# Three-product matmuls of an encoder block: the matmul on the weights' low part moved to the end of each K tile, and the K loop of a plain weight pair moved outside the loop over the accumulators

## The chip, the cores and the metric

The kernel runs on one core of a Trainium2 chip, as one program in one launch. The metric is the time of that program on the device, in microseconds (us). Each kernel's time is the median of several runs; the profile is taken of one execution by the hardware profiler.

## The reference

One layer of a bidirectional encoder, batch 1, 256 tokens, model width 2048, all in float32. Cut to what matters:

```python
h = rms_norm(x, g_mix)                       # x: 256 x 2048
c_q, c_kv, k_rope, dq, dk, dv = split(h @ w_in)
out_mla  = mla_attention(...)                # 8 heads, from c_q (512 wide), c_kv (256), k_rope (64)
out_diff = diff_attention(...)               # 4 heads, two softmaxes each, minus lam
x = x + concatenate([out_mla, out_diff]) @ w_out      # 2048 x 2048
x = x + cross_attention(rms_norm(x), rms_norm(mem))   # 4 heads into 256 memory tokens
hf = rms_norm(x, g_ffn)
x = x + (silu(hf @ w_gate) * (hf @ w_up)) @ w_down    # hidden width 5632
return rms_norm(x, g_final)
```

The inputs are random; no mask is used anywhere.

## The kernel before, in words

*Precision.* TensorE gets every operand as two float32r tiles, a high part `h` (the value rounded by a cast on ScalarE, L107) and a low part `l` (the value minus the high part, a subtraction on VectorE, L108). A product of two such operands is three matmuls into the same accumulator, written by `mm(o, l, r)`: high stationary x high moving (L99), high stationary x low moving (L100), low stationary x high moving (L101). The stationary operand is always a 128 x 128 block of activations, the moving one a 128 x 512 block of weights. In the names, `wh` and `wl` are the weights' high and low part, and `mixT_h`, `x2n_h`, `hT_h`, `forms_h` with their `_l` partners are activations.

*Wide projections.* The output projection, the gate, up and down products of the feed-forward part and their like run in `wide_project` (L254). It computes 256 tokens x 1024 columns in four accumulators of 128 x 512 in PSUM, `accs[tt][oc]`: tt is the half of the tokens, oc the half of the columns. The weights come in pairs of K tiles (two times 128 rows of 1024 columns), 1 MB a pair by one DMA into a tile `wraw` of a pool of three. `kinds` gives each pair a letter:

- A plain pair ("P") is split as two halves, one for each K tile, into `wh` and `wl` (pool `wp`, four buffers each). Then each accumulator takes its two K tiles, three matmuls each: 24 matmuls.
- A summed pair ("W") is computed with seven products in place of eight. VectorE adds blocks of the weights into `tsum` (L287, L291, L292), which are split too, and the activations have a set of prepared combinations, `forms` (`summed_pair`, L239: four small additions into `sums`, L245 to L248, and three splits). Four products go into extra PSUM tiles Q1, Q5, Q7, Q6 that are shared by all summed pairs of the projection, three go straight into an accumulator: 21 matmuls. After the last summed pair, `leave(Q)` takes the four Q tiles out of PSUM with one ScalarE copy and four VectorE additions or subtractions (L358 to L361 in `wide_add`).

`order` sets the order of the pairs in a projection. At its end, `join` combines each accumulator with what `leave` produced (VectorE, L340 in `wide_result`, L364 in `wide_add`). `wide_add` adds into the residual: its accumulators begin as a ScalarE copy of the residual (L261), which needs the PSUM bank free; the banks of accumulators and of Q tiles change places from one projection to the next (`banks.reverse()`).

```python
w = [split_blocks(raw[:, 2 * k:2 * k + 2, :]) for k in range(2)]   # plain pair, L271
for tt in range(NT):
    for oc in range(2):
        for k in range(2):
            mm(accs[tt][oc], pairs[i].at(k, tt), w[k][:, oc, :], ...)
```

*What sets the order.* The program is written in the order of the computation, and the Tile framework then schedules it with a timeline of its own (`schedule_with_timeline_sim=True`): each engine's instructions are put into a fixed list, in which a matmul may pass others of the source. On the chip an engine works off its list in order and waits, where it must, on semaphores. So both the code and the scheduler decide what stands behind what on TensorE (PE), VectorE (DVE) and ScalarE (ACT). The loads of `wraw` are issued by SyncE (SP) in program order.

*Stages in time.* Input projection and attention to about 230 us, output projection and cross-attention to about 460, then the feed-forward part: gate and up products of 1024 columns each, the hidden tile transposed by TensorE, and three groups of down projections of two halves each, the last of which ends the program with the final norm.

Of the kernel before, what the change touches and what calls it, by code (L numbers as in the profile page):

```python
# [15 lines left out]
AF = mybir.ActivationFunctionType  # L16
ALU = mybir.AluOpType
# [4 lines left out]
NT = S // P  # L22
# [16 lines left out]
GU_KINDS = "PPWPWPWP"  # L39

# [40 lines left out]
def encoder_block(ctx: ExitStack, tc: tile.TileContext, a, out):  # L81
    nc = tc.nc
# [14 lines left out]
    def mm(o, l, r, start, stop, seeded=False):  # L97

        nc.tensor.matmul(o, l.h, r.h, start=start, stop=False, skip_group_check=seeded)  # L99
        nc.tensor.matmul(o, l.h, r.l, start=False, stop=False, skip_group_check=seeded)  # L100
        nc.tensor.matmul(o, l.l, r.h, start=False, stop=stop, skip_group_check=seeded)  # L101

    last_split, last_cast = [None], [None]
# [119 lines left out]
    def split_blocks(src, pool=None):  # L223
        w = w_tile(src.shape[1], pool)
        split_into(w, src)
        return w
# [27 lines left out]
    def wide_project(pairs, src, order, kinds, leave, join, closed=(0, 1), before=None, seed=None):  # L254

        accs = [[acc_tile() for _ in range(2)] for _ in range(NT)]
# [7 lines left out]
        Q = {}  # L264
        for n, i in enumerate(order):
            stop = n == len(order) - 1
# [58 lines left out]
    def wide_result(pairs, src, order, kinds):  # L325
# [16 lines left out]
        wide_project(pairs, src, order, kinds, leave, join)  # L342
# [747 lines left out]
```

## Time and profile before

| quantity | value |
|---|---|
| time, median of 3 runs | 1142.07 us (1141.78 to 1142.09) |
| time of the profiled execution | 1141.65 us |
| its span | 1139.8 us |
| instructions in it | 14403 |
| mean granted TensorE clock | 0.998 of full speed |
| bytes moved by DMA | 222.13 MB, mean 195 GB/s |

The profiled execution is one more run; its time is 1.85 us above its span, the stretch from its first to its last recorded instruction. Busy time is the time in which an engine executes, not the time in which it is needed: an engine that is busy 85% of the span may never be what the others wait for. Weight loads (PEld) run on TensorE beside its matmuls, so the two shares of PE and PEld don't add up. In rows of single instructions the columns are start, length, engine, line of the kernel, operation, output <- inputs, with buffer numbers left out; a wait, where there is one, stands in brackets at the end with the partner that ended it. The row of the chain of waits gives what the end of the program hung on, followed back: PE for 98% of the span.

```profile
PE 98%; issue 1%; ACT 0%; DVE 0%; POOLq 0%; POOL 0%; ACTq 0%
```

### The profile page before, as it was taken

The numbers are of one execution on the slowest core, as the hardware profiler recorded it, in microseconds if no ns is written. First come the engines' busy times: TensorE is split into PE (matmuls) and PEld (weight loads), VectorE is DVE, ScalarE is ACT, GpSimd is POOL, SyncE is SP. The second block draws the span as 40 slices with busy tenths as digits, with TensorE's granted clock in tenths as the row PEclk, the third lists the DMA queues.
The fourth block names the chain that finished last, engine by engine and source line by source line (L and its number), as shares of the span: only waits on it lengthen the run. The fifth ranks groups of instructions, "written<-read, shape, count | busy, mean of one in ns | idle before, by whom it ended". The sixth has DMA issues, their size and how long they took to land.

```text
span 1139.8 us, 14403 instructions
## 1 busy us (share of the span) xinstructions
PE 1130.6 (99%) x5390; PEld 946.4 (83%) x5390; DVE 973.2 (85%) x1322; ACT 667.5 (59%) x965; POOL 58.6 (5%) x75
## 2 busy tenths in 40 slices
PE   9999999999999999999999999999999999999997
PEld 7888888888788888888888888888888888888886
DVE  7788766878896777989898988998998898999895
ACT  7755455567566555665565555565554564665663
POOL 5910000000001000000000000000000000000000
PEclk9999999999999999999999999999999999999999
DMA  9655333546567444455556556556555555565553
GB/s 362 241 195 185 124 125 139 181 149 224 191 227 259 156 161 179 161 211 189 212 194 219 185 191 218 185 190 216 185 187 220 201 205 190 191 247 196 195 181 129
DMA packets 35494, 222.13 MB, mean 195 GB/s; under 512 B 4321, under 2 KB 5601, under 8 KB 11105
## 3 DMA queue, kind: packets, MB, share of 16 engines
q1 hardware_dynamic: 33696, 216.60, 52.9%
q0 software_dynamic: 864, 3.15, 0.8%
q10 hardware_dynamic: 864, 1.47, 0.4%
q8 instruction: 42, 0.69, 0.2%
q14 instruction: 28, 0.22, 0.1%
HBM read 219.11 MB, written 2.10 MB: 194 GB/s over the span
## 4 chain that ended last, share of the span: by engine, by line
PE 98%; issue 1%; ACT 0%; DVE 0%; POOLq 0%; POOL 0%; ACTq 0%
PE acc L99 26%; PE acc L101 26%; PE acc L100 26%; PE q L100 4%; PE q L99 4%; PE q L101 4%; PE pt L502 2%; PE ppt L650 1%; PE psc L100 1%; PE psc L101 1%; PE psc L99 1%; PE acckv L99 0%; PE acckv L101 0%; PE acckv L100 0%; PE pt L922 0%
## 5 line engine op out<-in xcount | busy, mean ns | idle before, releaser
L107 ACT CAST wh<-wraw 128x1024 fp32r<-128x1024 f32 (+2 forms) x401 | 389.8, 989 | 283.2 <-PE acc L101 219.5
L108 DVE TENSOR_TENSOR wl<-wraw,wh 128x1024 fp32r<-128x1024 f32 (+2 forms) x401 | 455.3, 1148 | 88.8 <-ACT wh L107 86.8
L107 ACT CAST wh<-tsum 128x1024 fp32r<-128x1024 f32 (+1 forms) x98 | 98.0, 1006 | 73.1 <-PE acc L101 29.7
L108 DVE TENSOR_TENSOR wl<-tsum,wh 128x1024 fp32r<-128x1024 f32 (+1 forms) x98 | 113.6, 1165 | 19.5 <-ACT wh L107 19.5
L100 PE MATMUL acc<-wl,x2n_h 128*128 128x512 f32 x320 | 124.5, 390 | 0.0
L101 PE MATMUL acc<-wh,x2n_l 128*128 128x512 f32 x320 | 123.9, 389 | 0.0
L99 PE MATMUL acc<-wh,x2n_h 128*128 128x512 f32 x320 | 108.2, 390 | 0.0
L100 PE MATMUL acc<-wl,x0T_h 128*128 128x512 f32 x224 | 88.5, 395 | 0.0
L101 PE MATMUL acc<-wh,x0T_l 128*128 128x512 f32 x224 | 88.2, 394 | 0.0
L99 PE MATMUL acc<-wh,x0T_h 128*128 128x512 f32 x224 | 86.9, 396 | 0.0
L100 PE MATMUL q<-wl,forms_h 128*128 128x512 f32 x191 | 74.3, 389 | 0.0
L101 PE MATMUL q<-wh,forms_l 128*128 128x512 f32 x191 | 74.1, 389 | 0.0
L100 PE MATMUL acc<-wl,hT_h 128*128 128x512 f32 x188 | 73.3, 392 | 0.0
L101 PE MATMUL acc<-wh,hT_l 128*128 128x512 f32 x188 | 72.4, 389 | 0.0
L101 PEld LDWEIGHTS acc<-wh,x2n_l 128*128 128x128 f32 x320 | 60.1, 188 | 12.4
L100 PEld LDWEIGHTS acc<-wl,x2n_h 128*128 128x128 f32 x320 | 60.1, 188 | 12.3
L99 PEld LDWEIGHTS acc<-wh,x2n_h 128*128 128x128 f32 x320 | 59.9, 188 | 12.3
L99 PE MATMUL q<-wh,forms_h 128*128 128x512 f32 x191 | 66.7, 389 | 0.0
L99 PE MATMUL acc<-wh,hT_h 128*128 128x512 f32 x188 | 64.5, 391 | 0.0
L100 PE MATMUL acc<-wl,forms_h 128*128 128x512 f32 x162 | 62.5, 389 | 0.0
L101 PE MATMUL acc<-wh,forms_l 128*128 128x512 f32 x162 | 62.4, 389 | 0.0
L99 PE MATMUL acc<-wh,forms_h 128*128 128x512 f32 x162 | 61.3, 389 | 0.0
(402 smaller groups left out, 2247.9 us busy)
## 6 DMA issues: line engine op xcount, KB each, us to landing
wraw<-in_w_gate SPq DMA_DIRECT2D x44, 1024.0 KB, 4.8
wraw<-in_w_up SPq DMA_DIRECT2D x44, 1024.0 KB, 4.8
wraw<-in_w_dn SPq DMA_DIRECT2D x41, 1024.0 KB, 4.8
wraw<-in_w_in SPq DMA_DIRECT2D x24, 1024.0 KB, 4.8
wraw<-in_w_out SPq DMA_DIRECT2D x16, 1024.0 KB, 4.8
wraw<-in_w_in_lat SPq DMA_DIRECT2D x5, 832.0 KB, 7.2
wraw<-in_w_xk SPq DMA_DIRECT2D x4, 1024.0 KB, 5.4
wraw<-in_w_xq SPq DMA_DIRECT2D x4, 1024.0 KB, 5.9
```

Source lines behind the costliest of these rows:

```text
L99: nc.tensor.matmul(o, l.h, r.h, start=start, stop=False, skip_group_check=seeded)
L100: nc.tensor.matmul(o, l.h, r.l, start=False, stop=False, skip_group_check=seeded)
L101: nc.tensor.matmul(o, l.l, r.h, start=False, stop=stop, skip_group_check=seeded)
L107: last_cast[0] = nc.scalar.copy(out=dst.h, in_=src).ins
L108: last_split[0] = nc.vector.tensor_tensor(out=dst.l, in0=src, in1=dst.h.bitcast(F32), op=ALU.subtract).ins
L502: nc.tensor.transpose(out=pt[:, j * P:(j + 1) * P], in_=src[:, j * P:(j + 1) * P], identity=ident)
L650: nc.tensor.transpose(out=pt[:, kt * S + tt * P:kt * S + (tt + 1) * P], in_=p[:, tt, kt * P:(kt + 1) * P], identity=ident)
```

## The change

Three things, all in the order in which matmuls are written; the set of matmuls, casts, subtractions and transfers is the same.

1. `mm_late` takes a list of products. For each it writes high x high and low stationary x high moving, and only when the list is through, the matmuls that use the weights' low part. `mm` calls it with a list of one, so a single product now has its `wl` matmul last.
2. In a plain pair the loop over the two K tiles is the outer one. The list holds one K tile's products with all four accumulators: eight matmuls on `wh`, then four on `wl`, then the second K tile in the same way.
3. In a summed pair the seven products go as lists (Q1 and accumulator 01), (Q5 and Q7), accumulator 00, (Q6 and accumulator 10).

The diff also adds a second way to make the low part (a scaled copy on ScalarE and an accumulating DMA), for pairs named in `GU_CARRIED`. That tuple is empty, so no pair takes it.

```diff
+GU_CARRIED = ()
     def mm(o, l, r, start, stop, seeded=False):
-        nc.tensor.matmul(o, l.h, r.h, start=start, stop=False, skip_group_check=seeded)
-        nc.tensor.matmul(o, l.h, r.l, start=False, stop=False, skip_group_check=seeded)
-        nc.tensor.matmul(o, l.l, r.h, start=False, stop=stop, skip_group_check=seeded)
+        mm_late([(o, l, r, start, stop)], seeded)
+
+    def mm_late(products, seeded=False):
+        for o, l, r, start, stop in products:
+            nc.tensor.matmul(o, l.h, r.h, start=start, stop=False, skip_group_check=seeded)
+            nc.tensor.matmul(o, l.l, r.h, start=False, stop=False, skip_group_check=seeded)
+        for o, l, r, start, stop in products:
+            nc.tensor.matmul(o, l.h, r.l, start=False, stop=stop, skip_group_check=seeded)
...
-                w = [split_blocks(raw[:, 2 * k:2 * k + 2, :]) for k in range(2)]
-                for tt in range(NT):
-                    for oc in range(2):
-                        for k in range(2):
+                w = [split_blocks(raw[:, 2 * k:2 * k + 2, :], by_transfer=k == 1 and i in carried) for k in range(2)]
+                for k in range(2):
+                    products = []
+                    for tt in range(NT):
+                        for oc in range(2):
                             ends = stop or i == plain[-1] and tt == oc == 1
-                            mm(accs[tt][oc], pairs[i].at(k, tt), w[k][:, oc, :], not used[tt][oc],
-                               ends and k == 1 and oc in closed, seed is not None)
+                            products.append((accs[tt][oc], pairs[i].at(k, tt), w[k][:, oc, :], not used[tt][oc],
+                                             ends and k == 1 and oc in closed))
                             used[tt][oc] = True
+                    mm_late(products, seed is not None)
...
-            mm(Q[1], A11, b11[:, 0, :], *own)
-            mm(accs[0][1], S3, b11[:, 1, :], False, stop, seed is not None)
-            mm(Q[5], S5, t1, *own)
-            mm(Q[7], S7, t3, *own)
-            mm(accs[0][0], A12, b21[:, 0, :], False, stop, seed is not None)
-            mm(Q[6], S6, t2, *own)
-            mm(accs[1][0], A22, t4, False, stop, seed is not None)
+            seeded = seed is not None
+            mm_late([(Q[1], A11, b11[:, 0, :], *own), (accs[0][1], S3, b11[:, 1, :], False, stop)], seeded)
+            mm_late([(Q[5], S5, t1, *own), (Q[7], S7, t3, *own)], seeded)
+            mm(accs[0][0], A12, b21[:, 0, :], False, stop, seeded)
+            mm_late([(Q[6], S6, t2, *own), (accs[1][0], A22, t4, False, stop)], seeded)
```

After the change the lines of the matmuls are L106 (high x high), L107 (low stationary x high) and L109 (high stationary x low weights). Other lines keep their code and move: the split's cast L107 to L115 and its subtraction L108 to L116, the scaled subtraction L114 to L122, the small additions L245 to L248 to L258 to L261, the accumulators' seed L261 to L274, the additions of `tsum` L287, L291 and L292 to L302, L306 and L307, `leave` L358 to L361 to L371 to L374, the joins L340 and L364 to L353 and L377.

What the scheduler makes of it, at three places. The first is the second half of the output projection, where its accumulators acc_2990 to acc_2992 are used for the first time; wh_3000 and wh_3004 are the two K tiles of a plain pair. TensorE's list before:

```order
L99 MATMUL acc_2990<-wh_3000,mixT_h_1111 128x512
L99 MATMUL acc_2991<-wh_3000,mixT_h_1111 128x512
L100 MATMUL acc_2990<-wl_3001,mixT_h_1111 128x512
L101 MATMUL acc_2990<-wh_3000,mixT_l_1112 128x512
L99 MATMUL acc_2990<-wh_3004,mixT_h_1111 128x512
L100 MATMUL acc_2991<-wl_3001,mixT_h_1111 128x512
L101 MATMUL acc_2991<-wh_3000,mixT_l_1112 128x512
L99 MATMUL acc_2991<-wh_3004,mixT_h_1111 128x512
L99 MATMUL acc_2992<-wh_3000,mixT_h_1111 128x512
```

And after:

```order
L106 MATMUL acc_2990<-wh_3000,mixT_h_1111 128x512
L107 MATMUL acc_2990<-wh_3000,mixT_l_1112 128x512
L109 MATMUL acc_2990<-wl_3001,mixT_h_1111 128x512
L106 MATMUL acc_2990<-wh_3004,mixT_h_1111 128x512
L107 MATMUL acc_2990<-wh_3004,mixT_l_1112 128x512
L106 MATMUL acc_2991<-wh_3000,mixT_h_1111 128x512
L107 MATMUL acc_2991<-wh_3000,mixT_l_1112 128x512
L109 MATMUL acc_2991<-wl_3001,mixT_h_1111 128x512
L106 MATMUL acc_2991<-wh_3004,mixT_h_1111 128x512
L107 MATMUL acc_2991<-wh_3004,mixT_l_1112 128x512
L109 MATMUL acc_2990<-wl_3005,mixT_h_1111 128x512
L109 MATMUL acc_2991<-wl_3005,mixT_h_1111 128x512
```

Before, the third accumulator is begun in the ninth row from the pair's first. Now the first two accumulators take both K tiles ahead of it, and the next pair's (wh_3046 and wh_3050, twelve rows), and it is begun in the 25th. VectorE's list at this place, with the subtraction that frees the bank of that accumulator (`left` <- `left`, q7), before:

```order
L359 TENSOR_TENSOR left_2933<-q5_2774,left_2932 128x512
L114 SCALAR_TENSOR_TENSOR mT_l_3033<-xraw_3034,gains_101,mT_h_3032 128x256 x3
L108 TENSOR_TENSOR wl_3001<-wraw_2998,wh_3000 128x1024
L364 TENSOR_TENSOR xres0_111<-acc_2627,left_2931 128x512
L360 TENSOR_TENSOR left_2932<-left_2932,q7_2775 128x512
```

And after:

```order
L122 SCALAR_TENSOR_TENSOR mT_l_3033<-xraw_3034,gains_101,mT_h_3032 128x256 x4
L116 TENSOR_TENSOR wl_3005<-wraw_2998,wh_3004 128x1024
L377 TENSOR_TENSOR xres0_111<-acc_2627,left_2931 128x512
L372 TENSOR_TENSOR left_2933<-q5_2774,left_2932 128x512
L116 TENSOR_TENSOR wl_3047<-wraw_3044,wh_3046 128x1024
L116 TENSOR_TENSOR wl_3051<-wraw_3044,wh_3050 128x1024
L373 TENSOR_TENSOR left_2932<-left_2932,q7_2775 128x512
```

Two splits of the next pair, wl_3047 and wl_3051, now stand ahead of that subtraction.

The second place is the second half of the last down projection. wh_9733 is the last buffer of a summed pair, and wh_9743, the cast of a single block, goes into the buffer that wh_9733 leaves. TensorE before:

```order
L99 MATMUL acc_9686<-wh_9733,forms_h_8628 128x512
L99 MATMUL q1_9729<-wh_9733,forms_h_8628 128x512
L100 MATMUL q1_9729<-wl_9734,forms_h_8628 128x512
L101 MATMUL q1_9729<-wh_9733,forms_l_8629 128x512
L100 MATMUL acc_9686<-wl_9734,forms_h_8628 128x512
L101 MATMUL acc_9686<-wh_9733,forms_l_8629 128x512
```

Thirteen more rows with neither buffer follow, and the next is the first that uses wh_9743. After:

```order
L106 MATMUL acc_9686<-wh_9733,forms_h_8628 128x512
L107 MATMUL acc_9686<-wh_9733,forms_l_8629 128x512
L109 MATMUL acc_9686<-wl_9734,forms_h_8628 128x512
L106 MATMUL q1_9729<-wh_9733,forms_h_8628 128x512
L107 MATMUL q1_9729<-wh_9733,forms_l_8629 128x512
L109 MATMUL q1_9729<-wl_9734,forms_h_8628 128x512
L106 MATMUL acc_9685<-wh_9743,forms_h_8628 128x512
L107 MATMUL acc_9685<-wh_9743,forms_l_8629 128x512
```

Between wh_9733's last reader and wh_9743's first there is now one matmul.

The third place is the first group's down projection, where two summed pairs follow each other; forms_l_5411 is the low part of the second one's activations. VectorE before:

```order
L246 TENSOR_TENSOR sums_5412<-pt_5384,sums_5412 128x128
L247 TENSOR_TENSOR sums_5412<-pt_5384,a21_5413 128x128
L108 TENSOR_TENSOR wl_5552<-wraw_5535,wh_5551 128x512
L291 TENSOR_TENSOR tsum_5588<-tsum_5588,wraw_5582 128x512
L248 TENSOR_TENSOR sums_5412<-pt_5384,sums_5412 128x128
L108 TENSOR_TENSOR wl_5585<-wraw_5582,wh_5584 128x1024
L292 TENSOR_TENSOR tsum_5588<-tsum_5588,wraw_5582 128x512
L108 TENSOR_TENSOR forms_l_5411<-pt_5390,forms_h_5410 128x256
L108 TENSOR_TENSOR forms_l_5411<-pt_5384,forms_h_5410 128x256
L108 TENSOR_TENSOR forms_l_5411<-sums_5412,forms_h_5410 128x512
```

And after:

```order
L307 TENSOR_TENSOR tsum_5588<-tsum_5588,wraw_5582 128x512
L116 TENSOR_TENSOR wl_5585<-wraw_5582,wh_5584 128x1024
L258 TENSOR_TENSOR sums_5412<-a21_5413,pt_5390 128x128
L116 TENSOR_TENSOR wl_5591<-tsum_5588,wh_5590 128x1024
L259 TENSOR_TENSOR sums_5412<-pt_5384,sums_5412 128x128
L260 TENSOR_TENSOR sums_5412<-pt_5384,a21_5413 128x128
L116 TENSOR_TENSOR wl_5595<-wraw_5582,wh_5594 128x512
L261 TENSOR_TENSOR sums_5412<-pt_5384,sums_5412 128x128
L116 TENSOR_TENSOR forms_l_5411<-pt_5390,forms_h_5410 128x256
L116 TENSOR_TENSOR forms_l_5411<-pt_5384,forms_h_5410 128x256
L116 TENSOR_TENSOR forms_l_5411<-sums_5412,forms_h_5410 128x512
```

The splits wl_5591 and wl_5595 moved ahead of the low part of `forms`, the four small additions behind the split wl_5585, and the last addition of `tsum` (L307) ahead of it.

More of the change, by code (lines that the diff above doesn't have):

```diff
@@ L221, in w_tile, with split_blocks @@
             "p (b c) -> p b c", b=n) for x in tags])
-    def split_blocks(src, pool=None):
+    def split_blocks(src, pool=None, by_transfer=False):
         w = w_tile(src.shape[1], pool)
-        split_into(w, src)
+        if by_transfer:
+            nc.scalar.activation(w.l, src, AF.Copy, scale=-1.0)
+            last_cast[0] = nc.scalar.copy(out=w.h, in_=src).ins
+            nc.gpsimd.dma_start(out=w.l, in_=src, accum_op=ALU.add)
+        else:
+            split_into(w, src)
         return w
@@ L252, in summed_pair, with wide_project @@
         return Pair(forms=f)
-    def wide_project(pairs, src, order, kinds, leave, join, closed=(0, 1), before=None, seed=None):
+    def wide_project(pairs, src, order, kinds, leave, join, closed=(0, 1), before=None, seed=None, carried=()):
         accs = [[acc_tile() for _ in range(2)] for _ in range(NT)]
@@ L340, in join @@
             nc.vector.tensor_tensor(out=r, in0=acc, in1=r, op=ALU.subtract if (tt, oc) == (1, 0) else ALU.add)
-        wide_project(pairs, src, order, kinds, leave, join)
+        wide_project(pairs, src, order, kinds, leave, join, carried=GU_CARRIED)
         return res
```

## The prediction

> **What bounds the kernel now.** I read the page's busy times first, then busy times by stretch, then who waited for whom with TensorE's two rows apart, then the order of time at the places that the change moves. From the page:
>
> ```profile
> span 1139.8 us, 14403 instructions
> PE 1130.6 (99%) x5390; PEld 946.4 (83%) x5390; DVE 973.2 (85%) x1322; ACT 667.5 (59%) x965; POOL 58.6 (5%) x75
> ```
>
> A matmul's end is modelled, so 99% may hide short waits. The starts tell the pace. Five rows in order of time from the middle of an up product (start, length, engine, line), then busy times by stretch (start:end, length, busy time and count for PE, PEld, DVE, ACT, POOL, then the granted clock):
>
> ```profile
> 700.24 0.39 PE L101 MATMUL acc<-wh,x2n_l 128*128 128x512 f32 x1
> 700.46 0.39 PE L99 MATMUL acc<-wh,x2n_h 128*128 128x512 f32 x1
> 700.47 0.19 PEld L100 LDWEIGHTS acc<-wl,x2n_h 128*128 128x128 f32 x1
> 700.69 0.39 PE L100 MATMUL acc<-wl,x2n_h 128*128 128x512 f32 x1
> 700.92 0.39 PE L101 MATMUL acc<-wh,x2n_l 128*128 128x512 f32 x1
> ...
> 580.00:700.00 120.00, 120.00 (x531) 99.39 (x530) 109.08 (x122) 69.87 (x80) 0.00 (x0) 1.00 0.58 204
> 700.00:830.00 130.00, 130.00 (x591) 107.83 (x590) 120.63 (x151) 76.28 (x97) 0.00 (x0) 1.00 0.55 196
> 830.00:960.00 130.00, 130.00 (x575) 107.70 (x574) 115.97 (x128) 70.38 (x78) 0.00 (x0) 1.00 0.58 208
> 460.00:1080.00 620.00, 620.00 (x2780) 513.79 (x2779) 568.47 (x683) 360.97 (x439) 1.10 (x2) 1.00 0.56 200
> ```
>
> Starts lie 0.22 to 0.23 us apart, whatever the line. Two long stretches give the same pace as a mean: 120.00/531 = 0.226 and 130.00/575 = 0.226 us. (700 to 830 has shorter transposes in it.) So in these stages TensorE issues at its own pace without a hole, at a granted clock of 1.00. What can be saved is what it waits:
>
> ```profile
> PE acc L99 <- ACT acc L261: 0.8, 1, 0.8
> PE po L99 <- ACT val_h L113: 0.2, 1, 0.2
> PEld acc L99 <- ACT acc L261: 1.2, 1, 1.2
> PEld po L99 <- ACT val_h L113: 0.6, 1, 0.6
> PEld acc L99 <- ACT pT_h L107: 0.4, 1, 0.4
> PEld po L101 <- DVE val_l L114: 0.3, 1, 0.3
> PEld acc L100 <- DVE wl L108: 0.2, 1, 0.2
> ```
>
> The load rows hold the matmul rows' waits too: 1.2 + 0.6 + 0.4 + 0.3 + 0.2 = 2.7 us, all that TensorE lost to a named partner after its warm-up. The wait that the change loosens most directly, for the weights' low part (wl), is the last row: 0.2 us in 1140.
>
> **The change part by part.** It removes and adds no instruction: 5390 matmuls, each with its own load, before and after. A product's three matmuls (high x high, high stationary x low weights, low stationary x high weights) stay; what changes is their rank, and in a plain pair the loop over the two K tiles moves outside that over the four accumulators. 5390 times the same pace is the same time; the rest is waits.
>
> *Low part later, high part freed earlier, in every plain pair.* In the code a K tile now runs eight matmuls on its high part before the first on its low part: 8 x 0.226 = 1.8 us of cover, where one accumulator gave one or two matmuls. The wait that this could end is 0.2 us: counted as nothing. In return the low buffer is used to the tile's last matmul, one later than before (0.23 us); the buffer's next split has several microseconds of other tiles as cover, so nothing again. If that cover were gone, VectorE would hold its queue: the second rival.
>
> *All four accumulators end together.* At a projection's end the four joins come in a row instead of spread. One is 682 ns:
>
> ```profile
> L340 DVE TENSOR_TENSOR res<-acc,res 128x512 f32<-128x512 f32 x40 | 26.3, 682 | 0.4 <-PE acc L101 0.4
> ```
>
> Rows of that size start 0.60 us apart (below). At an up product's end the order sets, between the end of its first accumulator and the first transpose of the hidden tile, 41 PE rows, 9.3 us at 0.226; VectorE has four joins, one split and one multiplication there, 4 x 0.60 + 1.14 + 0.60 = 4.1 us. The down projection's first pairs cover it: nothing.
>
> *Place 1: second half of the output projection.* In order of time, TensorE and the two engines that it waits for:
>
> ```profile
> 286.08 0.62 PE L99 MATMUL acc<-wh,mixT_h 128*128 128x512 f32 x2
> 286.36 0.68 DVE L360 TENSOR_TENSOR left<-left,q 128x512 f32<-128x512 f32 x1
> 287.67 0.39 PE L99 MATMUL acc<-wh,mixT_h 128*128 128x512 f32 x1
> 288.18 0.58 ACT L261 COPY acc<-xres 128x512 f32<-128x512 f32 x1
> 288.81 0.50 PE L99 MATMUL acc<-wh,mixT_h 128*128 128x512 f32 x1 [0.75 <-ACT acc L261]
> ```
>
> The third accumulator is seeded by ScalarE (288.18 to 288.76) and TensorE starts on it at 288.81, 1.14 us after its last start: 0.91 lost. Afterwards this first use stands 24 rows behind the pair's first, 286.08 + 24 x 0.226 = 291.5. But in VectorE's order the subtraction that frees the bank (L360, now L373) moves behind two splits whose buffers TensorE frees only at about 286.1. The list from there (rest of the gains splits, a split, a join, a subtraction, two splits, then L373) gives an end near 291.2; with the copy's 0.58 and a handover of 0.05, 291.8. Lost: 0.3. So -0.6, with -0.9 (wait gone) and 0 as ends.
>
> *Place 2: second half of the last down projection.* A cast of a single block (wh_9743) goes into the buffer that wh_9733 leaves, in both builds. Before:
>
> ```profile
> 1093.14 0.39 PE L101 MATMUL acc<-wh,forms_l 128*128 128x512 f32 x1
> 1093.62 0.63 ACT L107 CAST wh<-wraw 128x512 fp32r<-128x512 f32 x1
> 1096.32 0.39 PE L99 MATMUL acc<-wh,forms_h 128*128 128x512 f32 x1
> ```
>
> The last reader of wh_9733 starts at 1093.14, the cast runs 1093.62 to 1094.25, and TensorE needs it at 1096.32: 2.1 us spare. In the new order only one matmul stands between that last reader and the first user: due 0.45 us after it, ready 0.48 + 0.63 + 0.05 = 1.16 us after it. +0.7 us. The ends are 0 (only if other work held TensorE by itself) and 1.1 (ScalarE busy with one more copy when the buffer comes free).
>
> *Place 3: two summed pairs in a row, first group's down projection.* VectorE rows, and the TensorE row that reads the last:
>
> ```profile
> 579.48 0.28 DVE L246 TENSOR_TENSOR sums<-pt,sums 128x128 f32<-128x128 f32 x1
> 579.68 0.28 DVE L247 TENSOR_TENSOR sums<-pt,a 128x128 f32<-128x128 f32 x1
> 579.88 0.68 DVE L108 TENSOR_TENSOR wl<-wraw,wh 128x512 fp32r<-128x512 f32 x1
> 580.48 0.68 DVE L291 TENSOR_TENSOR tsum<-tsum,wraw 128x512 f32<-128x512 f32 x1
> 581.28 1.22 DVE L108 TENSOR_TENSOR wl<-wraw,wh 128x1024 fp32r<-128x1024 f32 x1
> 582.41 0.68 DVE L292 TENSOR_TENSOR tsum<-tsum,wraw 128x512 f32<-128x512 f32 x1
> 583.02 0.74 DVE L108 TENSOR_TENSOR forms_l<-pt,forms_h 128x256 fp32r<-128x256 f32 x2
> 585.54 0.62 PE L101 MATMUL q<-wh,forms_l 128*128 128x512 f32 x2
> ```
>
> Starts give the pace: 0.20 us for 128x128, 0.60 for 128x512, 1.13 for 128x1024. The stationary's low part is ready at 583.76 and read at 585.77, the second of the merged row: 2.0 us spare. In the new order the split of 581.28 has the four small sums behind it instead of ahead (0.8), two more splits ahead of the low part (1.13 + 0.60), and the last addition ahead of it (0.60 earlier): start 581.28 - 0.8 + 0.6 = 581.08, and 581.08 + 2.48 - 0.6 + 0.8 + 1.73 = 585.5. TensorE reads it five rows earlier, 585.77 - 1.13 = 584.64. Lost: 0.8 us; ends 0 and 1.2 (another 0.4 of rounding on 25 rows).
>
> *Start and tail* keep their instructions; nothing.
>
> Sum: -0.6 + 0.7 + 0.8 = +0.9 us. The profiled execution took 1141.65, 1.85 beyond its span; with the sum, 1142.55. It lies 0.42 below the median of the three runs, 1142.07; on that median, 1143.0.
>
> [...] The order before often puts two matmuls with the same stationary block behind each other (L99, then L100), and the change parts them. The rows at 700.47 and 700.69 show that such a second matmul had its own load of 0.19 us and came at the usual pace, so nothing is lost by parting them. [...]
>
> **The rivals.**
> - Nothing to tell: places 2 and 3 are covered by waits that TensorE finds elsewhere, and place 1 goes. The scheduler's order before took the high matmuls of several accumulators first already, so little of the change is new. 1142.07 - 0.6 = 1141.5.
> - Slower, by VectorE: it is 568.47 of 620 us busy from 460 to 1080, so it can lose 51.5 us there before TensorE must wait.
>
> ```profile
> 460.00:1080.00 620.00, 357.89 (x319) 1.00 0.56 200
> DVE wl L108 <- ACT wh L107: 47.0, 79, 2.4
> ACT wh L107 <- PE acc L101: 146.7, 106, 3.7
> ```
>
> The first row counts the wl splits there (319), the second VectorE's waits for casts, the third ScalarE's for buffers. If every split were held 0.226 us for its low buffer, 319 x 0.226 = 72 us, 20.6 over the spare: 1162.7. It decides from 51.5/319 = 0.16 us a split on. For it: in-order queue, and all joins and sums stand behind a held split. Against it: casts wait for buffers longer than anything (146.7), and the high buffers now come free up to four matmuls earlier.
> - Slower, by more places like 2 and 3: over 2.3 us needs two or three more of 0.7. Against it: the schedule has no other buffer handed over within one matmul. 1145.0 or more.
> - Faster: all waits of the load rows go and none comes, 1142.07 - 2.7 = 1139.4. Against it: three of the five (po, val, pT) belong to attention, where the order hardly moves.
> - A stationary block saved its load before and not now: some 620 such neighbours x 0.19 = 118 us if nothing hid it, 1260. The rows above say no.
>
> **How the numbers follow.** 0.2% (2.3 us) is about what a measurement can tell. Likeliest, the sum: 0.59. Nothing to tell: 0.20. VectorE: 0.08. More places: 0.07. Faster: 0.05. Loads: 0.01. Same: 0.59 + 0.20 = 0.79; slower 0.16; faster 0.05. The likeliest's own range is -0.9 to +2.3 on 1142.07 (the terms' ends): 1141.2 to 1144.4. The range that leaves out at most 0.2 reaches down halfway to the faster case and up into the case of more places: 1140.6 to 1145.4.
>
> **What the changed profile would show.** PE pace 0.226 from 580 to 700 and 830 to 960; PE busy 99%. No row of some 0.8 us of PE waiting for ACT L274 near 289, or a shorter one; a new wait of 0.7 near 1093 on a cast, and one of 0.8 near 585 on forms_l. ScalarE's waits for PE smaller than the 146.7 above, VectorE's waits on PE for wl new but without a PE row. Wrong would be: PE rows waiting for wl or joins in every projection (VectorE), a pace other than 0.226, or a granted clock under 1.00.

## The result and the profile after

The changed kernel takes 1147.89 us, median of 4 runs (1145.84 to 1149.26), against 1142.08 for the kernel before (4 runs, 1141.78 to 1142.31). The ratio is 1.005, with a 95% interval of 1.0032 to 1.0067: slower by 0.5%, 5.8 us. The forecast was 1143.0 with a range to 1145.4: no change that can be told, and it was wrong. The runs of the changed kernel also spread over 3.4 us, those of the one before over 0.5; part of the reason is told below.

The profiled execution took 1148.27. The page's first lines:

```profile
span 1146.5 us, 14655 instructions
PE 1133.4 (99%) x5390; PEld 948.6 (83%) x5390; DVE 975.4 (85%) x1322; ACT 666.7 (58%) x965; POOL 58.2 (5%) x75
```

Each engine executes as many instructions as before, and its busy time differs by less than 3 us; the 252 further instructions of the count are of the kinds that aren't counted as busy (registers, branches, semaphores, DMA issues). The span is 6.7 us longer. Busy times by stretch (start:end, length, busy time and count of PE, PEld, DVE, ACT and POOL, then the granted clock, the busy share of the DMA engines and their GB/s):

```profile
580.00:700.00 120.00, 117.06 (x510) 96.43 (x509) 106.24 (x124) 67.36 (x80) 0.00 (x0) 0.99 0.55 196
700.00:830.00 130.00, 130.00 (x591) 107.95 (x590) 121.15 (x150) 74.81 (x94) 0.00 (x0) 1.00 0.56 199
830.00:960.00 130.00, 130.00 (x576) 107.66 (x575) 116.47 (x128) 74.41 (x84) 0.00 (x0) 1.00 0.57 204
```

From 700 to 960 nothing has changed: 591 and 576 matmuls, 591 and 575 before. From 580 to 700 there are 510 instead of 531: 21 x 0.226 = 4.7 us are lost in this one stretch. What TensorE waited for, after its warm-up:

```profile
PE q L106 <- ACT forms_h L115: 2.9, 1, 2.9
...
PE po L107 <- DVE val_l L122: 1.1, 2, 0.8
PE acc L106 <- ACT wh L115: 0.5, 1, 0.5
PE po L106 <- ACT val_h L121: 0.2, 1, 0.2
```

New are the waits for `forms_h`, for `val_l` and for `wh`: place 3, cross-attention and place 2. The 0.2 us for `val_h` stood in the profile before too.

**Place 3.** Rows of ScalarE, VectorE and TensorE in order of time (a bracket holds the idle time before and what ended it):

```profile
578.82 0.62 ACT L115 CAST wh<-wraw 128x512 fp32r<-128x512 f32 x1 [2.35 <-PE acc L107]
579.34 0.37 ACT L115 CAST forms_h<-pt 128x256 fp32r<-128x256 f32 x1
...
580.68 0.75 DVE L116 TENSOR_TENSOR forms_l<-pt,forms_h 128x256 fp32r<-128x256 f32 x2
...
582.55 1.22 DVE L116 TENSOR_TENSOR wl<-wraw,wh 128x1024 fp32r<-128x1024 f32 x1
...
583.55 0.39 PE L109 MATMUL q<-wl,forms_h 128*128 128x512 f32 x1
...
583.99 1.23 DVE L116 TENSOR_TENSOR wl<-tsum,wh 128x1024 fp32r<-128x1024 f32 x1
...
585.53 0.68 DVE L116 TENSOR_TENSOR wl<-wraw,wh 128x512 fp32r<-128x512 f32 x1
586.13 0.28 DVE L261 TENSOR_TENSOR sums<-pt,sums 128x128 f32<-128x128 f32 x1
...
586.45 0.37 ACT L115 CAST forms_h<-pt 128x256 fp32r<-128x256 f32 x1 [1.71 <-DVE sums L261]
...
586.87 0.50 PE L106 MATMUL q<-wh,forms_h 128*128 128x512 f32 x1 [2.94 <-ACT forms_h L115]
...
587.94 0.63 PE L107 MATMUL q<-wh,forms_l 128*128 128x512 f32 x1
...
588.37 0.63 PE L109 MATMUL q<-wl,forms_h 128*128 128x512 f32 x1
```

TensorE starts nothing from 583.55 to 586.87: 3.32 - 0.23 = 3.1 us lost. It waits for the high part of the second pair's forms. That cast reads a PSUM tile (`pt`) which VectorE's small sums read too, and starts 0.04 us after the last of them ends. VectorE comes to that sum so late because three splits (1.13 + 1.13 + 0.60 us) and the first pair's forms stand ahead. And after the wait TensorE is slow: starts 0.43 us apart instead of 0.23. The granted clock in these microseconds:

```profile
587.00:588.00 1.00, 1.00 (x4) 0.75 (x5) 0.91 (x2) 0.34 (x1) 0.00 (x0) 0.67 0.71 123
588.00:589.00 1.00, 1.00 (x4) 0.81 (x3) 0.07 (x1) 0.39 (x1) 0.00 (x0) 0.50 0.91 369
...
590.00:591.00 1.00, 1.00 (x4) 0.79 (x3) 0.95 (x2) 0.93 (x1) 0.00 (x0) 0.62 0.34 139
591.00:592.00 1.00, 1.00 (x6) 0.79 (x5) 1.00 (x1) 0.69 (x2) 0.00 (x0) 1.00 0.00 0
```

The clock falls to half behind the wait and is back before 591. Eleven starts from 586.87 on take until 591.09, 4.22 us where 11 x 0.2265 = 2.49 would do: 1.7 lost on top. Place 3 costs 4.8 us.

**Cross-attention.** `val` is the values' product, cast by ScalarE and split by VectorE in two pieces; `po` takes probabilities times values:

```profile
403.40 0.69 ACT L121 ACTIVATE val_h<-acc,rstdm 128x512 fp32r<-128x512 f32 x1 [1.23 <-PE acc L109]
...
403.99 1.04 ACT L115 CAST wh<-wraw 128x1024 fp32r<-128x1024 f32 x1
...
404.93 0.69 ACT L121 ACTIVATE val_h<-acc,rstdm 128x512 fp32r<-128x512 f32 x1
...
406.20 0.74 DVE L122 SCALAR_TENSOR_TENSOR val_l<-acc,rstdm,val_h 128x512 fp32r<-128x512 f32 x1
...
407.00 0.39 PE L107 MATMUL po<-pxT_h,val_l 128*128 128x256 f32 x1 [0.82 <-DVE val_l L122]
```

Here `val` is the stationary operand, so the change uses its low part second instead of third; and a weight's cast (403.99) stands between the two pieces of `val`, which ScalarE cast in a row before (1.31 us for both, from 403.72). The hundredth matmul after the first `po` starts 21.22 us after the last one ahead of it, 19.91 before: 1.3 us.

**Place 2** came as forecast: the cast into the freed buffer starts at 1099.22 and its user 0.05 us after its end.

```profile
1098.73 0.39 PE L107 MATMUL q<-wh,forms_l 128*128 128x512 f32 x1
...
1099.22 0.62 ACT L115 CAST wh<-wraw 128x512 fp32r<-128x512 f32 x1 [1.11 <-PE q L107]
...
1099.89 0.50 PE L106 MATMUL acc<-wh,forms_h 128*128 128x512 f32 x1 [0.54 <-ACT wh L115]
```

**Place 1** has no wait near 289 any more. The seed is copied from 290.22 (0.59 us) and first used, 24 rows after the pair's first at 286.38, at 291.82: 1.0 us to spare, where the forecast had left 0.3 us of wait.

The starts of the same matmul by number, counted from TensorE's first, add it up:

| matmul number | before, us | after, us | difference | what lies between |
|---|---|---|---|---|
| 200 | 41.17 | 41.80 | +0.63 | the first microseconds (below) |
| 2050 | 398.23 | 397.99 | -0.24 | place 1 and two late starts (below): -0.9 |
| 2700 | 539.47 | 540.44 | +0.97 | cross-attention: +1.2 |
| 4900 | 1031.03 | 1036.83 | +5.80 | place 3: +4.8 |
| 5389 | 1132.50 | 1139.15 | +6.65 | place 2: +0.85 |

The first 0.63 is not the change's. In the traces' record of the granted clock the full clock begins 5.7 us after the first instruction in the profile before and 7.1 us in the one after, and the first experiment below, with the order of before up to 580 us, lies 0.65 behind there too (the same matmul at 580.75, before at 580.10). The -0.9 has three parts: place 1 gave 1.0, a start that came 0.3 late at 280.51 in the profile before is late no more, and a new late one at 328.14, behind ScalarE's copy out of PSUM, took 0.4 back.

One of the eleven executions of the kernel with all three places mended (below) took 2956.07 us at a granted clock of 1.00; it is left out of that kernel's ratio, the median without it is 1141.62, and its cause is open.

### The profile page after: what moved, and what is told of

It is laid out like the page before. It is cut to its first block, busy times and chain, and to the rows that moved or that the text cites. A ratio compares the mean times of both kernels' runs of the same rounds, so it can differ in the third digit from the quotient of the medians.

```text
span 1146.5 us, 14655 instructions
## 1 busy us (share of the span) xinstructions
PE 1133.4 (99%) x5390; PEld 948.6 (83%) x5390; DVE 975.4 (85%) x1322; ACT 666.7 (58%) x965; POOL 58.2 (5%) x75
## 4 chain that ended last, share of the span: by engine, by line
PE 98%; issue 1%; ACT 1%; DVE 0%; POOLq 0%; POOL 0%; ACTq 0%
PE acc L106 26%; PE acc L107 26%; PE acc L109 26%; PE q L106 4%; PE q L107 4%; PE q L109 4%; PE pt L515 2%; PE ppt L663 1%; PE psc L109 1%; PE psc L107 1%; PE psc L106 1%; PE acckv L106 0%; PE acckv L109 0%; PE acckv L107 0%; PE pt L935 0%
## 5 line engine op out<-in xcount | busy, mean ns | idle before, releaser
L115 ACT CAST wh<-wraw 128x1024 fp32r<-128x1024 f32 (+2 forms) x401 | 389.8, 989 | 295.1 <-PE acc L107 228.8
L116 DVE TENSOR_TENSOR wl<-wraw,wh 128x1024 fp32r<-128x1024 f32 (+2 forms) x401 | 455.9, 1149 | 98.9 <-ACT wh L115 91.4
L115 ACT CAST wh<-tsum 128x1024 fp32r<-128x1024 f32 (+1 forms) x98 | 98.3, 1008 | 76.5 <-PE acc L107 33.3
L106 PE MATMUL acc<-wh,x2n_h 128*128 128x512 f32 x320 | 124.7, 390 | 0.0
L107 PE MATMUL acc<-wh,x2n_l 128*128 128x512 f32 x320 | 123.4, 389 | 0.0
L116 DVE TENSOR_TENSOR wl<-tsum,wh 128x1024 fp32r<-128x1024 f32 (+1 forms) x98 | 113.6, 1166 | 8.4 <-ACT wh L115 6.6
L109 PE MATMUL acc<-wl,x2n_h 128*128 128x512 f32 x320 | 94.7, 390 | 0.0
L106 PE MATMUL acc<-wh,x0T_h 128*128 128x512 f32 x224 | 88.6, 396 | 0.0
L107 PE MATMUL acc<-wh,x0T_l 128*128 128x512 f32 x224 | 88.4, 395 | 0.0
L109 PE MATMUL acc<-wl,x0T_h 128*128 128x512 f32 x224 | 86.4, 394 | 0.0
L106 PE MATMUL q<-wh,forms_h 128*128 128x512 f32 x191 | 74.7, 392 | 2.9 <-ACT forms_h L115 2.9
L107 PE MATMUL q<-wh,forms_l 128*128 128x512 f32 x191 | 74.9, 393 | 0.0
L107 PE MATMUL acc<-wh,hT_l 128*128 128x512 f32 x188 | 72.7, 390 | 0.0
L106 PE MATMUL acc<-wh,hT_h 128*128 128x512 f32 x188 | 72.7, 390 | 0.0
L106 PEld LDWEIGHTS acc<-wh,x2n_h 128*128 128x128 f32 x320 | 60.1, 188 | 12.4
L107 PEld LDWEIGHTS acc<-wh,x2n_l 128*128 128x128 f32 x320 | 60.1, 188 | 12.3
L109 PEld LDWEIGHTS acc<-wl,x2n_h 128*128 128x128 f32 x320 | 59.9, 188 | 12.3
L109 PE MATMUL q<-wl,forms_h 128*128 128x512 f32 x191 | 69.6, 391 | 0.0
L106 PE MATMUL acc<-wh,forms_h 128*128 128x512 f32 x162 | 63.3, 392 | 0.5 <-ACT wh L115 0.5
L107 PE MATMUL acc<-wh,forms_l 128*128 128x512 f32 x162 | 63.0, 389 | 0.0
L109 PE MATMUL acc<-wl,forms_h 128*128 128x512 f32 x162 | 60.8, 389 | 0.0
L302 DVE TENSOR_TENSOR tsum<-wraw 128x1024 f32<-128x1024 f32 x44 | 53.7, 1220 | 3.7 <-DMA wraw<-in_w_up 1.9
```

Of the source, the lines that this page charges most:

```text
L107: nc.tensor.matmul(o, l.l, r.h, start=False, stop=False, skip_group_check=seeded)
L109: nc.tensor.matmul(o, l.h, r.l, start=False, stop=stop, skip_group_check=seeded)
L115: last_cast[0] = nc.scalar.copy(out=dst.h, in_=src).ins
L116: last_split[0] = nc.vector.tensor_tensor(out=dst.l, in0=src, in1=dst.h.bitcast(F32), op=ALU.subtract).ins
L302: nc.vector.tensor_tensor(out=t[:, 0:2, :], in0=raw[:, 1:3, :], in1=raw[:, 0:1, :].to_broadcast([P, 2, 512]), op=ALU.add)
```

## The experiments

Theory A: the loss is the sum of these places, and of the 4.8 us at place 3 the 1.7 behind the wait are a fall of the clock that the wait brings. Theory B: every product, or every projection, pays a little. All kernels below were timed in five rounds against the kernel before on the same chip.

| experiment | median, us | before, us | ratio, 95% interval |
|---|---|---|---|
| before, with place 3's order of VectorE from after | 1147.37 | 1142.17 | 1.0043 (1.0029 to 1.0057) |
| after, place 3 half mended on VectorE | 1144.96 | 1142.17 | 1.0026 (1.0015 to 1.0037) |
| after, place 3 mended on VectorE | 1144.21 | 1142.17 | 1.0019 (1.0010 to 1.0027) |
| after, low part of `val` last | 1148.38 | 1142.17 | 1.0054 (1.0042 to 1.0067) |
| before, with the new order of single products | 1143.31 | 1142.11 | 1.0011 (1.0002 to 1.0019) |
| before, with the new plain pairs | 1148.00 | 1142.11 | 1.0053 (1.0040 to 1.0066) |
| before, with the new summed pairs | 1142.40 | 1142.11 | 1.0002 (0.9993 to 1.0011) |
| after, all three places mended | 1141.63 | 1142.11 | 0.9996 (0.9987 to 1.0005) |
| before, short wait at place 3 | 1143.59 | 1141.99 | 1.0015 (1.0006 to 1.0024) |
| before, middle wait | 1145.95 | 1141.99 | 1.0029 (1.0020 to 1.0039) |
| before, long wait | 1149.53 | 1141.99 | 1.0066 (1.0053 to 1.0078) |

### Place 3 alone, put into the kernel before

An ordering edge that carries no wait puts three of the second summed pair's small sums behind the splits of its weights; `sums` holds those four instructions, `behind` adds the edges.

```diff
+    def behind(sums, *splits):
+        for a, b in zip((sums[0], sums[1], sums[3]), splits):
+            tc.add_manual_dep(a, b.name, ...)          # order on VectorE only
...
-            b11 = split_blocks(raw[:, 1:3, :])
+            b11 = split_blocks(raw[:, 1:3, :]); first_split = last_split[0]
...
-                t13 = split_blocks(t[:, 0:2, :])
-                b21 = split_blocks(raw[:, 3:4, :])
+                t13 = split_blocks(t[:, 0:2, :]); t13_split = last_split[0]
+                b21 = split_blocks(raw[:, 3:4, :]); i == hold and behind(pairs[i].s, first_split, t13_split, last_split[0])
```

> The kernel before, with one thing taken over from the changed kernel: at place 3 (first group's down projection, first half) VectorE splits the second summed pair's weights ahead of that pair's small sums, as in the changed kernel. Nothing else of the change is in it; the order of TensorE moves by some two dozen rows at that place. Theory A (the change lost its time at place 3: the cast of forms_h waits for the last small sum, TensorE waits for the cast, and a wait near 3 us is followed by matmuls at half the clock): the last small sum moves from 581.1 to about 585.1 us, TensorE would wait 2.0 to 2.7 us there, and if the clock falls another 1.7: 1144.1 to 1146.5. Theory B (the time is lost all over the kernel, by buffers of the low part held longer): no change, 1142.1.

1147.37: +5.2 us, nearly as much as the change's whole loss, from ordering edges on VectorE at this one place (the scheduler moved rows of TensorE and ScalarE around them). TensorE's row, and the clock behind it:

```profile
586.77 0.50 PE L99 MATMUL q<-wh,forms_h 128*128 128x512 f32 x1 [3.14 <-ACT forms_h L107]
```
```profile
587.00:591.00 4.00, 4.00 (x12) 3.13 (x12) 1.04 (x3) 1.33 (x3) 0.00 (x0) 0.57 0.75 262
```

Theory B falls here as the explanation of the loss: the kernel has neither the new loops nor the new order of the three matmuls. The time is above A's range, since the wait was 3.1 and not 2.0 to 2.7 us.

### Place 3 taken back in the changed kernel, in two steps

The splits of t13 and b21 (half), or also that of b11 (all), go behind the second pair's forms on VectorE:

```diff
-            b11 = split_blocks(raw[:, 1:3, :])
+            with tc.issue_after(pairs[i].last) if i == hold else ExitStack(): b11 = split_blocks(raw[:, 1:3, :])    # second step only
...
+                with tc.issue_after(pairs[i].last) if i == hold else ExitStack():
+                    t13 = split_blocks(t[:, 0:2, :]); b21 = split_blocks(raw[:, 3:4, :])
```

> The changed kernel; at place 3 two of the three splits that stand ahead of the second summed pair's small sums on VectorE (1.13 + 0.60 us) go behind that pair's forms. Theory A: the wait of 2.94 us shrinks by 1.73 to about 1.2, and with a wait that short the clock stays: 1147.9 - 1.7 - 1.7 = 1144.5. If the clock falls whatever the wait, 1146.2. Theory B: 1147.9.

> The changed kernel; at place 3 all three splits (1.13 + 1.13 + 0.60 us) go behind the second summed pair's forms. Theory A: the wait of 2.94 us and the half clock after it (1.7) go: 1147.9 - 4.6 = 1143.3, and the times spread no more than those of the kernel before. Theory B: 1147.9.

```profile
584.97 0.50 PE L106 MATMUL q<-wh,forms_h 128*128 128x512 f32 x1 [1.20 <-ACT forms_h L115]
```
```profile
582.39 1.05 ACT L115 CAST wh<-tsum 128x1024 fp32r<-128x1024 f32 x1 [1.50 <-PE acc L107]
583.35 0.36 ACT L115 CAST forms_h<-pt 128x256 fp32r<-128x256 f32 x1
583.61 0.62 ACT L115 CAST wh<-wraw 128x512 fp32r<-128x512 f32 x1
...
584.23 0.50 PE L106 MATMUL q<-wh,forms_h 128*128 128x512 f32 x1 [0.79 <-DVE forms_l L116]
```

1144.96 and 1144.21. The half step takes 1.7 us off the wait and, in the profiled execution, the fall of the clock with it (1.00 from 585 to 589): 2.9 us in all. The full step leaves 0.8 us of wait where A expected none: with VectorE mended the forms are still late, because ScalarE has casts of weights ahead of the second pair's forms and between them. The one at 582.39 waits 1.50 us for its buffer, and only then comes the first cast of these forms. The theory had one engine too few.

### The low part of val last again

```diff
-                mm(po[:, j * S:(j + 1) * S], v[:, kt, ...], pTs[j][:, kt, :], kt == 0, kt == NT - 1)
+                mm(po[:, j * S:(j + 1) * S], v[:, kt, ...], pTs[j][:, kt, :], kt == 0, kt == NT - 1, weights_late=False)
```

> The changed kernel, but in the product of the attentions' values and probabilities (the helper that writes po) the matmul on the values' low part is third again, as before. Theory A: in cross-attention TensorE waits 0.28 + 0.82 us for val_l in the changed kernel and 0.2 in the kernel before, with the steps around it 1.3 us in all: 1147.9 - 1.3 = 1146.6. Rival: the scheduler's order of the cast of wh ahead of the second val_h keeps the wait, 1147.9.

1148.38: no gain, and the rival holds. ScalarE's cast of a weight stays between the two pieces of `val`, so TensorE now waits for the second high part and the second low part in turn; where the low part stands among the three matmuls of `po` isn't what costs the time:

```profile
405.33 0.39 PE L100 MATMUL po<-pxT_h,val_h 128*128 128x256 f32 x1 [0.23 <-ACT val_h L121]
...
406.66 0.39 PE L100 MATMUL po<-pxT_h,val_l 128*128 128x256 f32 x1 [0.60 <-DVE val_l L122]
```

### The three parts of the change, each alone

The kernels are made from the changed one, with the code of before in the other parts.

> One part of the change alone: a single product's matmul on the moving operand's low part is third (the input projection, attention and the other projections outside the wide ones); the wide projections keep the loops and the three matmuls in the order of the kernel before. Theory A (the sum of a few places, each with its own wait): of the places only cross-attention is in this kernel, +1.2 us: 1143.4. Theory B (every product pays): about a quarter of the products are in it, 1142.2 + 1.4 = 1143.6, with no wait of 0.8 us for val_l.

> One part of the change alone: in a plain pair the loop over the K tiles is outside that over the four accumulators, with the low part's four matmuls last in each K tile; all else in the order of the kernel before. The lists of VectorE and ScalarE at place 3 come out nearly as in the changed kernel, and so do the seed at place 1 and the buffer at place 2. Theory A: -1.1 (place 1) + 4.9 (place 3) + 0.8 (place 2): 1146.8, most of the loss. Theory B: its share by the number of products, +3: 1145.

> One part of the change alone: the summed pairs' products in lists of two with the low part's matmuls last; all else in the order of the kernel before. Theory A: neither place 2 nor place 3 nor cross-attention has the new order; at place 1 the third accumulator is begun 21 rows after the first instead of 8, so its wait of 0.9 goes: 1141.3, at most 1142.2. Theory B: its share of the products, +1.4: 1143.6.

The order of single products: 1143.31, too near to both theories' numbers to decide between them; the waits do. Its TensorE waits for `val` as the changed kernel does, and still for the seed at place 1:

```profile
PE po L110 <- DVE val_l L125: 1.1, 2, 0.8
PE acc L104 <- ACT acc L277: 0.7, 1, 0.7
```

The plain pairs: 1148.00, 5.9 us and as much as the whole change. It has place 3, place 2 and two more waits for a cast of a weight than the changed kernel. One at 762 us is of the kind of place 2: the cast itself waits 1.32 us for TensorE to leave the buffer. The other, at 319 us in the output projection, is not: ScalarE reaches that cast late, behind activations that waited 3.03 us for a transfer of the memory tokens. By the starts the two cost 1.1 and 1.3 us in the profiled execution, which at 1149.34 lies 2.5 above A's number; the median lies 1.2 above it:

```profile
PE q L101 <- ACT forms_h L116: 2.6, 1, 2.6
PE acc L101 <- ACT wh L116: 1.5, 2, 0.8
...
PE acc L107 <- ACT wh L116: 1.0, 1, 1.0
```

The summed pairs: 1142.40, no change that can be told, and not the gain of 0.8 that A expected. The wait at place 1 shrinks to 0.2 us, but another of 0.4 comes near 329, for ScalarE's copy of Q1 out of PSUM:

```profile
PE acc L101 <- ACT left L371: 0.4, 1, 0.4
PE acc L101 <- ACT acc L275: 0.2, 1, 0.2
```

### All three places mended

The second step above, and: the casts of weights held behind the casts of `forms` on ScalarE too; the next weights' casts and splits held behind both pieces of `val`; at place 2 the product that uses wh_9743 issued after the others of its pair.

```diff
-                b21 = split_blocks(raw[:, 3:4, :])
+                with tc.issue_after(pairs[i].cast) if hold and i in (hold, hold - 1) else ExitStack(): b21 = split_blocks(raw[:, 3:4, :])
...
-        accs = project(lambda kt: xoT[:, kt, :], [a["w_xo"][oc, 0]])
+        with tc.issue_after(xv_parts[0]) if oc == 1 else ExitStack(), tc.issue_after(xv_parts[1]) if oc == 1 else ExitStack(): accs = project(...)
...
-            mm(accs[0][0], A12, b21[:, 0, :], False, stop, seeded)
+            late or mm(accs[0][0], A12, b21[:, 0, :], False, stop, seeded)
...
+            if late:
+                with tc.issue_after(last_mm[0]): mm(accs[0][0], A12, b21[:, 0, :], False, stop, seeded)
```

> The changed kernel with the order mended at three places: at place 3 ScalarE and VectorE make the forms of both summed pairs ahead of the casts and splits that had moved ahead of them; in cross-attention the two casts of val stand together, ahead of the next weights' casts; at place 2 the product that uses wh_9743 comes after the others of its pair. Theory A: 1147.9 - 4.9 - 1.1 - 0.8 = 1141.1, between 1140.8 and 1142.0: what is left of the change is the gain at place 1, and it can't be told from the kernel before. Theory B: 1146 or more.

1141.63: 6.3 us below the changed kernel, with its loops and its orders of matmuls kept but for the one product at place 2. Against the kernel before the interval spans 1; it can't be told from it. TensorE's waits and the stretch that had lost 21 matmuls:

```profile
PE po L107 <- DVE val_l L122: 0.3, 1, 0.3
PE po L106 <- ACT val_h L121: 0.2, 1, 0.2
```
```profile
580.00:700.00 120.00, 120.00 (x532) 99.34 (x531) 109.45 (x125) 70.71 (x82) 0.00 (x0) 1.00 0.59 212
```

Place 2 is mended only in part. No wait for the cast is left, but between 1092.21 and 1093.97 four starts come late by 0.6 us in all. Against matmul 200, which starts 0.21 us earlier than in the profile before, matmul 4900 has gained 0.7 us and the last one 0.1.

### How the clock depends on the wait

The first experiment again, with less or more of VectorE's work ahead of the last small sum. Short: `((sums[0], splits[0]), (splits[1], sums[3]))` as the edges. Middle: both `sums[0]` and `sums[3]` behind the first split only. Long: the split of b21 three more times, with the same values.

> The kernel before with VectorE's order at place 3 so changed that only the split of 1.13 us (and not those of 1.13 + 0.60 behind it) stands ahead of the second summed pair's small sums: a wait of about 3.14 - 1.73 = 1.4 us in place of the 3.14 of the first experiment. If the granted clock falls after a wait only when the wait is long, the time is 1142.1 + 1.6 = 1143.7, with the clock at 1.00 after the wait, and now and then a run 1.5 higher. If it falls after any wait over 1 us: 1145.4 in all runs.

> The same with the split of 0.60 us alone behind the last small sum: a wait of about 3.14 - 0.60 = 2.5 us. If the chance that the clock falls grows with the wait: 1142.1 + 2.7 = 1144.8 in the runs without the fall and 1146.5 in those with it, some of both. If the fall has nothing to do with the wait: 1144.8 in all.

> The same order as in the first experiment, with VectorE's last split of the four repeated three times (1.8 us, the same values again): a wait of about 4.9 us. If a longer wait makes the fall sure and costs the same 1.7 once: 1142.1 + 5.1 + 1.7 = 1148.9 in all runs. If the time at half clock grows with the wait: 1150 or more.

For each the TensorE row after the wait, then a microsecond behind it:

```profile
584.69 0.50 PE L99 MATMUL q<-wh,forms_h 128*128 128x512 f32 x1 [1.34 <-ACT forms_h L107]
```
```profile
587.00:588.00 1.00, 1.00 (x6) 0.83 (x5) 0.00 (x0) 0.67 (x1) 0.00 (x0) 1.00 0.54 156
```
```profile
585.68 0.50 PE L99 MATMUL q<-wh,forms_h 128*128 128x512 f32 x1 [2.15 <-ACT forms_h L107]
```
```profile
587.00:588.00 1.00, 1.00 (x3) 0.75 (x3) 0.09 (x1) 0.00 (x0) 0.00 (x0) 0.50 0.60 188
```
```profile
588.84 0.79 PE L99 MATMUL q<-wh,forms_h 128*128 128x512 f32 x1 [5.32 <-ACT forms_h L107]
```
```profile
590.00:591.00 1.00, 1.00 (x4) 0.81 (x3) 0.03 (x1) 0.00 (x0) 0.00 (x0) 0.50 0.84 352
```

After 1.34 us of wait the clock stays in the profile, and all 11 times lie between 1143.36 and 1144.64. After 2.15 us the 9 times make two groups, three from 1143.93 to 1144.54 and six from 1145.83 to 1146.29: the same kernel costs some 2 us more in most of its executions, and the profiled one, at 1146.28, has the half clock. After 5.32 us all five lie at 1149.2 to 1150.2, 7.5 above before. In the profile 5.5 us of that are lost starts and 1.5 the half clock, which began 0.5 us before the wait ended; the other 0.5 lies ahead of 85 us. So by their times none of the 11, six of the nine and all five runs had the fall, and its price did not grow from 2.15 to 5.32 us of wait (1.7 and 1.5 us in the profiles). This explains part of the spread of the changed kernel's runs, whose wait was 2.94 in the profile: the one run at 1145.84 had a mean granted clock of 0.999, the others 0.995 to 0.997. The run at 1149.26 lies 1.4 above the median, at 0.995, and why is open.

## Why the prediction was wrong

**What bounds the kernel** held: away from the places TensorE keeps its pace of 0.226 us (700 to 960 above), and its waits, with the clock behind them, move the time. VectorE as the bound, the loads and theory B are excluded by the mended kernel, which has nearly all of the new order and the time of before.

**The step that failed is place 3, by size.** The prediction had the right place, wrote 0.8 us with ends 0 and 1.2, and it cost 4.8. Three things were left out.

- It followed the low part of the forms through VectorE's list and took their high part as given. The high part is what TensorE reads first, and its cast waits for VectorE's last small sum: neither reads what the other writes, but both read the same PSUM tile. The trace of before had this among the waits of ScalarE, in a row that the prediction did not read:

```profile
ACT forms_h L107 <- DVE sums L248: 2.0, 2, 1.4
```

  The traces show the order and not its reason: the cast begins 0.04 us after the sum ends in the changed kernel (586.13 + 0.28, then 586.45), and 0.03 before (581.08 + 0.28, then 581.39).
- It carried over ScalarE's list from before. That list had changed too: a cast of a weight block (wh_5551) went ahead of the first pair's forms and waited 2.35 us for its buffer, so VectorE reached everything at this place later: the first two pieces of the low part were ready at 587.28 and not at 585.5 (1.0 of that had been lost ahead of this place). The second step of mending, which left 0.8 us, and the kernel with all places mended, which took that away, show that ScalarE's casts of weights had a part of their own.
- It gave a wait its length as its price. In most executions with a wait of 2.15 us or more there was, by their times, a second price, the half clock: 1.5 us in the profile with the long wait, 1.7 in those of the changed kernel and of the middle wait.

**"Attention, where the order hardly moves"** was wrong: +1.3 us in cross-attention, and 1.2 for the order of single products by itself. The low part of `val` did move ahead in `po`, but with it third again the time stayed (1148.38). What cost was ScalarE's list: with the new order of single products a weight's cast stands between the two pieces of `val`, and with the pieces cast in a row again the waits shrank from 1.1 and 0.2 to 0.3 and 0.2.

**Places 1 and 2** were right in kind. Place 2: +0.7 forecast, 1099.89 - 1098.96 - 0.23 = 0.70 measured, and 0.1 more on the next start. Place 1: -0.6 forecast; no wait was left there at all, -1.0, since VectorE was through 1 us earlier than the forecast had it (290.19, not 291.2). The two other late starts, which the sum did not have, made -0.9 of it.

**The chance of more places** was priced at 0.07, for two or three more waits of 0.7 of the kind of place 2, "no other buffer handed over within one matmul". The loss came from waits of another kind: TensorE's, for casts and splits of activations. ScalarE's own waits for weights' buffers stood behind them at place 3.

A wait of 3.1 us as place 3's end would have taken the upper end of the terms only to 1142.07 + 0 + 1.1 + 3.1 = 1146.3. To reach 1147.89 the half clock had to be among the ends too (+1.7, 1148.0), and the wait needed the high part and ScalarE's list as well as VectorE's.

## What to carry to other kernels

Where TensorE has no holes, a reordering that is neutral on paper is worth the sum of the few waits that the scheduler adds and takes away: for each tile that TensorE reads late, follow every engine's list that leads to it, high part and low part, not only the one that moved most. A wait of TensorE may cost more than its length; here slow matmuls behind the waits of 2.15 to 5.32 us mostly cost 1.5 to 1.7 us more. When a change loses this way, mend the order at the places (here edges at three places gave back 6.3 us) before the idea is given up, and then see whether anything is left of its gain. Here 0.7 us was left by the starts up to place 2 and 0.1 behind it, which the times can't tell from nothing.

## What the runs showed of the hardware

In these profiles the granted clock fell after TensorE had been idle for 2.15 us (the middle wait: 0.50 from 587 to 589), 2.60 (the plain pairs: mean 0.55 from 587 to 590), 2.94 (the changed kernel: 0.50 from 588 to 590), 3.14 (the first experiment: mean 0.57 from 587 to 591) and 5.32 (the long wait: 0.50 from 589 to 591); after 1.20 (place 3 half mended) and 1.34 (the short wait) it stayed at 1.00, from 580 to 600. Taking the upper group of each kernel's times for the falls, six of nine runs had one with 2.15 us, three of four with 2.94, four of five with 3.14, all five with 5.32, and none of the 11 with 1.34 or of the 11 with 0.79. Two of the seven runs with 1.20 lie 1.1 to 1.3 us above the highest of the other five, at a mean clock of 0.997 where those have 0.998 or 0.999, and two of the eleven with the order of single products alone (longest wait behind the warm-up 0.8) lie 0.8 to 1.2 above the rest at 0.996 and 0.997; no profile caught one, and whether the clock fell in them stays open. The half clock lasted 3.41 us in the changed kernel (587.34 to 590.76), with starts 0.43 us apart in place of 0.23, and 3.4 with the middle and the long wait (twice what the stretches from 586 to 590 and from 588 to 592 lack of the full clock). Apart from the clock, the start behind a wait took 0.33 to 0.34 us in place of 0.23 (288.81 to 289.14 before, 1099.89 to 1100.22 after, 584.69 to 585.03 with the short wait), so these waits cost about 0.1 us more than their length.

The traces' record of the clock shows more for the kernels before and after. In the changed kernel the full clock lasted 580.27 us, the half clock 3.413 and the full clock behind it 552.96; in the kernel before, whose profile has no fall, the full clock lasted 1129.81. The three lengths at full clock are 170.0, 162.0 and 331.0 times the 3.413; why, the two traces do not show. What parts the two groups of times of the kernel with the middle wait isn't shown either.
